# mLSTM on Trainium2: a head's first values and keys begun in the third chunk of the head in front, the second pair's in the first chunk, GLA scans of the last heads behind the gate

## The chip, the cores and the metric

The kernel runs on one core of a Trainium2 chip. The metric is device time in microseconds (us) of one launch, the median of three runs. The engines are named as in the profile: PE (TensorE) with PEld for its weight loads, DVE (VectorE), ACT (ScalarE), POOL (GpSimd), SP (SyncE, which issues the DMAs). Each engine runs its instructions strictly in the order in which they stand in its queue; between engines there are semaphores.

## The reference, cut to what matters

A layer with one projection, two groups of heads and one output projection, on 2048 tokens of width 1024, in float32:

```python
u = rms_norm(x, norm_g)
q_g, k_g, v_g, z_g, r_g, x_m, z_m = split(u @ w_in)
log_a = log_sigmoid(r_g @ w_gla_gate_up + b_gla_gate) / 16      # GLA: 4 heads, dk 128, dv 256
S_t = diag(a_t) S_{t-1} + k_t^T v_t ;  o_g = q_t S_t            # in chunks, b = cumsum(log_a)
o_g = rms_norm(o_g) * silu(z_g)
c_act = silu(causal_conv4(x_m))                                 # mLSTM: 4 heads of 256
q_m, k_m = headwise(c_act, ..), headwise(c_act, ..);  v_m = headwise(x_m, ..)
C_t = f C_{t-1} + i v k^T ;  n_t = f n + i k                    # running-max stabiliser
h_m = C_t q_t / max(|n_t . q_t|, 1)
o_m = (rms_norm(h_m) + mlstm_skip * c_act) * silu(z_m)
return rms_norm(x + concat[o_g, o_m] @ w_out)
```

The cumulative sum of the gates is the `scan` of the text below; `v`, `v1l`, `ctk`, `ctl` are values and keys of the mLSTM.

## The kernel before

Tokens go in four blocks (`b`) of 512, each of four chunks (`c`) of 128. The first stretch of the span, to about 700 us, is the mLSTM of all four blocks; then comes the GLA of all four blocks, to about 1380, then the output projection. A product in float32 is made of three matmuls: each operand is split into a high part and a low part (`uh`/`ul`, `whi`/`wlo`, `v`/`v1l`, `ctk`/`ctl`), the high part by a cast on ACT, the low part by a subtraction on DVE or POOL.

The projections (`pp`, in the GLA part also `pv`) are a long stream of matmuls. PE's order is written out by hand by a small model: generators for the heads' work are advanced between pieces of the stream, `yield x` asks for x us of stream before the next step, `yield "name"` waits until that name is set. At most two heads of the mLSTM are open at a time. `od.wait()` and `od.hold(t)` model a pair of PSUM banks: `hold(t)` says how long after this step its bank is taken to be in use, and `wait` puts stream work ahead until the older of the two banks is taken to be free.

These two banks (`ps_t`, tag `pt`) carry in turn `pqp` (a head's queries), `pma` (its scores), `pmv` (values of a pair of chunks), `pmc` (transposed keys of a pair), and `pt` (the closing transposes of a pair, in `fin_pair`). A tile can be written once the tile two before it has been read. The readers are: of `pma` the scores' split (`A`, lines 788 to 790, ACT, DVE and POOL); of `pmv` `v` on ACT (853) and `v1l` on DVE (854), one of each for each chunk of the pair; of `pmc` `ctk` on ACT (869) and `ctl` on DVE (870); of `pt` two DVE steps into `ost` (805, 806).

A head is `mattn(b, h)` (line 809). After queries and scores it makes the values and keys of its first pair of chunks, `prep_v(0)` and `prep_c(0)`, once the head in front is done; then it goes through its four chunks. In a chunk: the split of the state, `C` (898 on ACT, 899 on DVE); two state updates `pmu` with their DVE step `Tm` (909); the output `pmo`; the split query `qx` of the next chunk (`prep_q`, ACT and POOL); and the norm: `dn`, `r`, a reciprocal on DVE (920 to 922), `jk` with its sum on ACT (925), `rsa` on DVE (220), `rs` on POOL (221), `rs` on DVE (928), `on` on ACT (931). In chunk 0 the second pair's values are made (`prep_v(1)`), in chunk 1 its keys (`prep_c(1)`); chunk 2 is the first to use both. The first head of a block takes its gates from `pkg` and `G` (735).

Order on the other engines is set by a scheduler with priorities (`ahead(tc, ...)`, `at(tc, ...)`), and where `after([...])` stands, as written.

In the GLA part `ggates` makes for each head four scans (1080), one for each chunk, and a copy of the last values `blast` (1083); `z` is gated by `th` (ACT, 580) and `zs` (DVE, 581), whose bank the stream's first `pv` matmul takes over; `zdone[b, 1]` is the `zs` of the block's second tile. One scan, the first of head 2, is ordered after it.

Of the kernel before, what the change touches and what calls it, by code (L numbers as in the profile page):

```python
# [25 lines left out]
H = 4  # L26
# [60 lines left out]
@contextmanager  # L87
def ahead(tc, n):

    tc.cur_priority -= n  # L90
    yield
    tc.cur_priority += n


def at(tc, n):
    def wrap(f):
        def g(*a):
            with ahead(tc, n):
                return f(*a)
        return g  # L100
    return wrap
# [58 lines left out]
def fast_path(ctx, tc, inside, xT, x, w_fm, w_v, w_r, wqT, wkT, wvT, wv, wg, w_up, b_g,  # L160
              norm_g, gla_g, conv_w, conv_b, b_if, ml_g, skip, w_out, fin_g, out):
    nc = tc.nc
    od = Order(tc)
# [646 lines left out]
    def mattn(b, h):  # L810
# [19 lines left out]
            for e in range(2):  # L830
                mm(pa[:, cs], cm[2 * h + e][:, cs], qp[:, e, cs], e == 0, e == 1)
        A = asplit(pa)
        od.hold(0.00)
        yield f"gr{b}"
        wk, wkh, wkl, ga, fl = gts[b]
        if h not in Tm:
# [37 lines left out]
        @at(tc, HPQ)  # L874
        def prep_q(c):
            if c < NC and (b or c):
                qx[c] = gp.tile([P, 2, 2, P], F32R, name="qx", tag="ca", bufs=2)
                split(qx[c][:, 0], qx[c][:, 1], qp[:, :, c * P:(c + 1) * P], QX)

        if (b, h) != (0, 0):  # L880
            yield f"mm{b}_{h - 1}" if h else f"mm{b - 1}_{H - 1}"
        yield from od.wait()
        prep_q(0)
        prep_v(0)
        od.hold(1.80)
        yield from od.wait()
        prep_c(0)
        od.hold(1.10)
        yield 2.10
        on = {}  # L890
        for c in range(NC):
            cs = slice(c * P, (c + 1) * P)
            first = b == 0 and c == 0
            last = b == NB - 1 and c == NC - 1
            if not first:
                Ch, Cl = (gp.tile([P, 2, 258], F32R, name="C", tag="C", bufs=2) for i in range(2))
                with ahead(tc, HPX):
                    nc.scalar.activation(Ch, T, AF.Copy, scale=ga[:, c, h:h + 1])
                    nc.vector.scalar_tensor_tensor(Cl, T, ga[:, c, h:h + 1], Ch.bitcast(F32), op0=ALU.mult, op1=ALU.subtract)
            v1, ctk = kv[c]  # L900
            if not last:
                for e in range(2):
                    pu = ps_u.tile([P, 258], F32, name="pmu", tag="pu")
                    mm3(pu, (ctk[0][:, e, :], ctk[1][:, e, :]), v1, True, True)
                    with ahead(tc, HPT):
                        if first:
                            nc.scalar.copy(T[:, e, :], pu)
                        else:
                            nc.vector.scalar_tensor_tensor(T[:, e, :], T[:, e, :], ga[:, c, h:h + 1], pu, op0=ALU.mult, op1=ALU.add)
                yield 0  # L910
            po = ps_o.tile([P, 258], F32, name="pmo", tag="po")
            mm3(po, (A[:, c, :], A[:, NC + c, :]), v1, True, first)
            if not first:
                for e in range(2):
                    mm3(po, (qx[c][:, 0, e, :], qx[c][:, 1, e, :]), (Ch[:, e, :], Cl[:, e, :]), False, e == 1)
            prep_q(c + 1)
            with ahead(tc, HPN):
                r = sp.tile([P, 1], F32, name="r", bufs=4)
                dn = sp.tile([P, 1], F32, name="dn")
                nc.vector.tensor_scalar(dn, po[:, DV:DV + 1], -1.0, fl[:, c, h:h + 1], op0=ALU.mult, op1=ALU.max)  # L920
                nc.vector.tensor_tensor(r, dn, po[:, DV:DV + 1], op=ALU.max)
                nc.vector.reciprocal(r, r)
                jk = sp.tile([P, DV], BF16, name="jk", bufs=1)
                ss = sp.tile([P, 1], F32, name="ss", bufs=4)
                nc.scalar.activation(jk, po[:, 0:DV], AF.Square, scale=r, accum_out=ss)
                rs = sp.tile([P, 1], F32, name="rs", bufs=4)
                rsqrt(rs, ss, DV)
                nc.vector.tensor_tensor(rs, rs, r, op=ALU.mult)
                o = gp.tile([P, DV], F32, name="on", bufs=4)
                if MON:  # L930
                    nc.scalar.activation(o, po[:, 0:DV], AF.Copy, scale=rs)
                else:
                    nc.vector.tensor_scalar(o, po[:, 0:DV], rs, None, op0=ALU.mult)
            on[c] = o
            yield 0.20
            if c < 2:
                yield from od.wait()
                (prep_v, prep_c)[c](1)
                od.hold(2.10)
            if c < NC - 1:  # L940
                yield 1.90
        od.done.add(f"mm{b}_{h}")
# [101 lines left out]
    def ggates(b):  # L1044
        yield (f"r{b}")
        yield 0.96
        yield from od.wait()
        prr = ps_t.tile([P, TB], F32, name="prr", tag="pt")
        for t in range(NC):
            tr(prr[0:16, t * P:(t + 1) * P], rts[b][:, t, :])  # L1050
        nc.vector.tensor_copy(rstk[0:16, :], prr[0:16, :])
        nc.vector.tensor_copy(rstk[64:80, :], rstk[0:16, :].bitcast(F32))
        nc.vector.tensor_tensor(rstk[32:48, :], prr[0:16, :], rstk[0:16, :].bitcast(F32), op=ALU.subtract)
        od.hold(1.70)
        yield 1.50
        prs = [gq.tile([P, 2, TB + 4], F32, name=f"bc{p}", tag=f"x{p}") for p in range(2)]
        for h in range(H):
            yield from od.wait()
            pg = ps_t.tile([P, TB], F32, name="pg", tag="pt")
            mm(pg, upk[:, h * P:(h + 1) * P], rstk, True, True)  # L1060
            nc.vector.tensor_scalar(prs[h // 2][:, h % 2, :TB], pg, bg[:, h:h + 1], -GCLIP, op0=ALU.add, op1=ALU.max)
            od.hold(0.98)
            yield 0
        chain = []
        for p in range(2):
            w = prs[p][:, :, :TB]
            chain.append(nc.scalar.activation(w, w, AF.Exp, scale=-1.0, accum_out=esum[:, b, p:p + 1]))
        for p in range(2):
            w = prs[p][:, :, :TB]
            chain.append(nc.scalar.activation(w, w, AF.Ln, bias=1.0))  # L1070
        after(chain)
        yield GY0
        for h in range(H):
            if h == 2 and f"za{b}_1" not in od.done:
                yield f"za{b}_1"
            w = prs[h // 2][:, h % 2, :TB]
            w3 = w.rearrange("p (c t) -> p c t", t=P)
            with ahead(tc, HYG):
                for c in range(NC):
                    sc = nc.vector.tensor_tensor_scan(w3[:, c], ones, w3[:, c], 0.0, op0=ALU.mult, op1=ALU.add)  # L1080
                    if h == 2 and c == 0:
                        after([zdone[b, 1], sc])
                nc.vector.tensor_copy(blast[:, b, h, :].unsqueeze(2), w3[:, :, P - 1:P])
            bc[b, h] = w
            od.done.add(f"gg{b}_{h}")
            yield GY1
# [694 lines left out]
```

## Time and profile before

| | |
|---|---|
| median of 3 runs | 1698.77 us (1696.33 to 1699.51) |
| profiled execution, its own time | 1694.07 us |
| its span | 1691.8 us |
| mean granted clock of PE | 0.989 |
| PE / PEld busy | 95% / 80% of the span |
| DVE / ACT / POOL busy | 56% / 41% / 26% |
| PE matmuls | 8840 |

Times in the rows are microseconds from the start of the span. Matmuls are pipelined: the length of a row runs into the next one, so the pace is read from start to start. What stands in brackets at the end of a row is the idle time of the engine before it and what ended that idle time. The granted clock of PE is 1.00 at 2.4 GHz and 0.50 at 1.2 GHz.

### The profile page before, as it was taken

What the parts mean: (1) busy time and instruction counts of PE and PEld (TensorE: products, weight loads), DVE (VectorE), ACT (ScalarE), POOL (GpSimd) and SP (SyncE); (2) the same over time, 40 slices, a digit from 0 to 9 for tenths busy, and PEclk for the clock granted to TensorE, in tenths of its full rate; (3) what the DMA queues carried; (4) which work ended last, traced back from release to release, by engine and by line L of the source; (5) the groups of instructions that cost most, each with busy time, mean ns of one, the idle gap of its engine ahead of it and who ended that gap; (6) DMA issues with size and microseconds to landing.
All of it is one profiled execution on the core that took longest, in us unless ns stands there. A gap on an engine that the chain in (4) does not pass through costs nothing.

```text
span 1691.8 us, 25558 instructions
## 1 busy us (share of the span) xinstructions
PE 1613.0 (95%) x8840; PEld 1354.0 (80%) x8840; DVE 954.7 (56%) x2125; ACT 695.3 (41%) x1486; POOL 444.9 (26%) x422
## 2 busy tenths in 40 slices
PE   7989899999999999899999999999999999999997
PEld 5767777877888788788888988888889877887775
DVE  4966776775667576834442434233523556567663
ACT  4666754554555455413231323132422433243331
POOL 3434321220121024344302120302031214223330
PEclk9999999999999999999999999999999999999999
DMA  8677667636664766666868586758575575573441
GB/s 268 200 266 241 230 219 236 199 107 211 200 199 145 221 196 203 213 241 202 301 212 298 187 299 202 255 175 288 194 261 193 175 250 195 168 249 133 163 144 65
DMA packets 221258, 355.42 MB, mean 210 GB/s; under 512 B 24368, under 2 KB 58160, under 8 KB 221120
## 3 DMA queue, kind: packets, MB, share of 16 engines
q1 hardware_dynamic: 221120, 353.70, 62.9%
q8 instruction: 72, 1.18, 0.3%
q14 instruction: 66, 0.54, 0.1%
HBM read 253.86 MB, written 102.89 MB: 211 GB/s over the span
## 4 chain that ended last, share of the span: by engine, by line
PE 45%; DVE 5%; DMA 3%; issue 3%; ACT 2%; POOL 2%; SPq 0%; POOLq 0%; DVEq 0%; ACTq 0%
PE py L191 16%; PE pp L191 16%; PE pv L191 9%; PE po L191 2%; DVE bc L1080 1%; PE pu L191 1%; DMA wlo<-w_dr 1%; PE pt L201 1%; PE pa L191 1%; POOL ring L1217 1%; DMA f<-q_dr 0%; DMA ring<-in_w_out 0%; DMA whi<-w_dr 0%; DVE as L215 0%; DVE yh L1312 0%
## 5 line engine op out<-in xcount | busy, mean ns | idle before, releaser
L191 PE MATMUL pp<-uh,whi 128*128 128x512 f32 x1008 | 420.8, 417 | 12.7 <-ACT whi L214 6.1
L191 PE MATMUL pp<-uh,wlo 128*128 128x512 f32 x1008 | 400.6, 397 | 0.2 <-POOL wlo L215 0.2
L191 PE MATMUL pp<-ul,whi 128*128 128x512 f32 x1008 | 400.3, 397 | 0.5 <-DVE ul L404 0.4
L191 PEld LDWEIGHTS pp<-uh,whi 128*128 128x128 f32 x1008 | 192.3, 191 | 53.0 <-ACT whi L214 6.1
L191 PEld LDWEIGHTS pp<-uh,wlo 128*128 128x128 f32 x1008 | 191.4, 190 | 47.6 <-DMA wlo<-w_dr 0.9
L191 PEld LDWEIGHTS pp<-ul,whi 128*128 128x128 f32 x1008 | 191.9, 190 | 39.7 <-issue 4.5
L215 POOL TENSOR_TENSOR wlo<-wraw,whi 128x512 fp32r<-128x512 f32 (+1 forms) x97 | 133.8, 1385 | 158.0 <-ACT whi L214 54.4
L1217 POOL TENSOR_TENSOR ring<-ring,ring 128x512 f32<-128x512 f32 x77 | 106.2, 1384 | 240.6 <-DMA ring<-in_w_out 112.4
L191 PE MATMUL pv<-whi,uh 128*128 128x256 f32 (+1 forms) x512 | 148.9, 291 | 10.6 <-DVE zs L581 8.5
L191 PE MATMUL pv<-wlo,uh 128*128 128x256 f32 (+1 forms) x512 | 145.6, 284 | 0.8 <-DMA wlo<-w_dr 0.5
L191 PE MATMUL pv<-whi,ul 128*128 128x256 f32 (+1 forms) x512 | 145.6, 284 | 0.0
L191 PE MATMUL py<-f,as 128*128 128x512 f32 x540 | 134.2, 400 | 8.7 <-DVE yf L1312 3.9
L214 ACT CAST as<-ring 128x512 fp32r<-128x512 f32 x105 | 65.0, 621 | 168.7 <-PE py L191 117.8
L191 PEld LDWEIGHTS py<-f,as 128*128 128x128 f32 x540 | 103.1, 192 | 34.3 <-ACT f L214 8.5
L215 POOL TENSOR_TENSOR qx<-qp,qx 128x256 fp32r<-128x256 f32 x60 | 55.7, 931 | 272.0 <-ACT qx L214 272.0
L191 PEld LDWEIGHTS pv<-whi,uh 128*128 128x128 f32 x512 | 97.1, 190 | 13.3 <-DVE zs L581 9.3
L191 PEld LDWEIGHTS pv<-wlo,uh 128*128 128x128 f32 x512 | 97.0, 189 | 1.9 <-DMA wlo<-w_dr 1.8
L191 PEld LDWEIGHTS pv<-whi,ul 128*128 128x128 f32 x512 | 97.2, 190 | 0.7
L215 DVE TENSOR_TENSOR as<-ring,as 128x512 fp32r<-128x512 f32 x105 | 85.2, 814 | 12.9 <-ACT as L214 12.2
L645 DVE SCALAR_TENSOR_TENSOR c<-xm,cw,c 128x512 f32<-128x512 f32 x96 | 78.2, 822 | 14.1 <-ACT c L643 13.4
L221 POOL TENSOR_TENSOR grs<-rsa,nhalf 128x2 f32<-128x2 f32 x32 | 23.4, 732 | 199.0 <-DVE rsa L220 177.8
L985 DVE TENSOR_TENSOR vl<-pv,v 128x256 fp32r<-128x256 f32 x56 | 23.5, 422 | 79.6 <-ACT v L983 79.6
(341 smaller groups left out, 3151.0 us busy)
## 6 DMA issues: line engine op xcount, KB each, us to landing
whi<-w_dr SPq DMA_DIRECT2D x212, 256.0 KB, 3.8
wlo<-w_dr SPq DMA_DIRECT2D x212, 256.0 KB, 4.2
wraw<-in_w_fm SPq DMA_DIRECT2D x80, 256.0 KB, 4.1
w_dr<-whi SPq DMA_DIRECT2D x76, 256.0 KB, 3.4
w_dr<-wlo SPq DMA_DIRECT2D x76, 256.0 KB, 3.3
o_dr<-ost SPq DMA_DIRECT2D x64, 256.0 KB, 3.4
ring<-o_dr SPq DMA_DIRECT2D x60, 256.0 KB, 3.1
ul<-u_dr SPq DMA_DIRECT2D x56, 256.0 KB, 4.3
```

Source lines behind the costliest of these rows:

```text
L191: nc.tensor.matmul(o, l, r, start=start, stop=stop, **k)
L201: nc.tensor.transpose(o, i, ident)
L214: nc.scalar.copy(hi, raw)
L215: (nc.gpsimd if "l" in pool else nc.vector).tensor_tensor(lo, raw, hi.bitcast(F32), op=ALU.subtract)
L221: nc.gpsimd.tensor_tensor(dst, a, nhalf.broadcast_to(list(src.shape)), op=ALU.pow)
L645: nc.vector.scalar_tensor_tensor(ca, xt[:, 1 + j:1 + j + TB], cw[:, t, j:j + 1], ca, op0=ALU.mult, op1=ALU.add)
L985: nc.vector.tensor_tensor(vl[b, h][t // 2][:, t % 2, :], pv[:, :DV], vv[b, h][:, t, :].bitcast(F32), op=ALU.subtract)
L1080: sc = nc.vector.tensor_tensor_scan(w3[:, c], ones, w3[:, c], 0.0, op0=ALU.mult, op1=ALU.add)
L1217: nc.gpsimd.tensor_tensor(o, a, b, op=ALU.subtract)
```

## The change

Four edits; the instructions of every engine stay the same in kind and number.

1. The second pair's values and keys are both made in chunk 0 (before: values in chunk 0, keys in chunk 1).
2. A head's first values and keys may start once the chunk 2 of the head in front has been written out (name `mp`), not only when that head is done (name `mm`). The first split query, `prep_q(0)`, comes after the head in front is done.
3. The hold of the scores' bank goes from 0.00 to 2.60, those of values and keys from 1.80, 1.10 and 2.10 to 2.20.
4. In `ggates` all scans of heads 2 and 3 are ordered after `zdone[b, 1]`, where before only the first scan of head 2 was.

```diff
         A = asplit(pa)
-        od.hold(0.00)
+        od.hold(2.60)
...
+        front = f"{b}_{h - 1}" if h else f"{b - 1}_{H - 1}"
         if (b, h) != (0, 0):
-            yield f"mm{b}_{h - 1}" if h else f"mm{b - 1}_{H - 1}"
+            yield "mp" + front
         yield from od.wait()
-        prep_q(0)
         prep_v(0)
-        od.hold(1.80)
+        od.hold(2.20)
+        yield 0
         yield from od.wait()
         prep_c(0)
-        od.hold(1.10)
+        od.hold(2.20)
         yield 2.10
+        if (b, h) != (0, 0) and "mm" + front not in od.done:
+            yield "mm" + front
+        prep_q(0)
...
-            if c < 2:
-                yield from od.wait()
-                (prep_v, prep_c)[c](1)
-                od.hold(2.10)
+            if c == 0:
+                for prep in (prep_v, prep_c):
+                    yield from od.wait()
+                    prep(1)
+                    od.hold(2.20)
+                    yield 0
+            if c == 2:
+                od.done.add(f"mp{b}_{h}")
...
-                    if h == 2 and c == 0:
+                    if h > 1:
                         after([zdone[b, 1], sc])
```

What this does to the order is shown at three places. The first is PE in the first head of block 1. Before, the second pair's keys (`pmc_3187`) stand one chunk's output behind `pmo_3152` of chunk 1, and `pmu_3209` of chunk 2 follows after nine stream matmuls:

```order
L191 MATMUL pmo_3152<-C_3138,qx_3079 128x258
L191 MATMUL pp_3108<-uh4_1786,whi_2969 128x512
...
L201 MATMUL pmc_3187<-ident_71,c0_2207 128x128
L201 MATMUL pmc_3187<-ident_71,c1_2219 128x128
...
L191 MATMUL pp_3108<-uh7_1830,whi_2969 128x512
L191 MATMUL pp_3108<-ul7_1831,whi_2969 128x512
L191 MATMUL pp_3108<-uh7_1830,wlo_2970 128x512
L191 MATMUL pmu_3209<-v1_3117,ctk_3188 128x258
L191 MATMUL pmu_3209<-v1l_3118,ctk_3188 128x258
L191 MATMUL pmu_3209<-v1_3117,ctl_3189 128x258
```

In after the same head has the values (`pmv_3119`) and keys (`pmc_3132`) of the second pair in chunk 0, then chunk 1 (`pmu_3158`, `pmo_3168`), and only then `pmu_3237` of chunk 2:

```order
L191 MATMUL pmv_3119<-wvs_124,xm0_2224 128x128 x4
L201 MATMUL pmc_3132<-ident_71,c0_2229 128x128
L201 MATMUL pmc_3132<-ident_71,c1_2241 128x128
...
L191 MATMUL pp_3063<-uh2_1737,whi_2906 128x512
...
L191 MATMUL pmu_3158<-v1_3022,ctk_3035 128x258
...
L191 MATMUL pmo_3168<-v1_3022,A_2839 128x258
...
L191 MATMUL pp_3063<-uh5_1861,whi_2969 128x512
...
L191 MATMUL pmu_3237<-v1_3120,ctk_3133 128x258
L191 MATMUL pmu_3237<-v1l_3121,ctk_3133 128x258
L191 MATMUL pmu_3237<-v1_3120,ctl_3134 128x258
```

So a whole chunk has moved between the keys and their first use. On ACT, at the same place, before had the cast `ctk_3188` behind `jk_3170` of chunk 1's norm:

```order
L898 ACTIVATE C_3205<-Tm0_1111,ga_2911 128x516
L214 CAST qx_3229<-qp_2773 128x256
L925 ACTIVATE jk_3170,ss_3171<-pmo_3152,r_3165 128x256
L869 CAST ctk_3188<-pmc_3187 128x512
L931 ACTIVATE on_3178<-pmo_3152,rs_3173 128x256
L580 ACTIVATE th_3248<-pp_3108 128x512
```

In after (whose lines from 880 on are numbered a few higher) the cast is `ctk_3133`:

```order
L929 ACTIVATE jk_3106,ss_3107<-pmo_3088,r_3101 128x256
L853 ACTIVATE v1_3120<-pmv_3119,wk_2931 128x256
L869 CAST ctk_3133<-pmc_3132 128x512
L935 ACTIVATE on_3114<-pmo_3088,rs_3109 128x256
L853 ACTIVATE v1_3120<-pmv_3119,wk_2931 128x256
L902 ACTIVATE C_3233<-Tm0_1114,ga_2934 128x516
```

It stands between the norm steps of chunk 0 and among the two value casts of its pair. The second place is PE at the change from that head to the next one. Before, the new head's values (`pmv_3342`) and keys (`pmc_3361`) follow the last output of the old head (`pmo_3298`) and the first closing transposes (`pt_3330`), and the second `pt_3376` comes after them:

```order
L191 MATMUL pmo_3298<-C_3284,qx_3229 128x258
...
L201 MATMUL pt_3330<-ident_71,on_3095 128x128 x2
L201 MATMUL pt_3330<-ident_71,on_3178 128x128 x2
L191 MATMUL pmv_3342<-wvs_124,xm1_2412 128x128 x4
...
L201 MATMUL pmc_3361<-ident_71,c2_2417 128x128
L201 MATMUL pmc_3361<-ident_71,c3_2518 128x128
...
L201 MATMUL pt_3376<-ident_71,on_3245 128x128 x2
L201 MATMUL pt_3376<-ident_71,on_3321 128x128 x2
```

In after they stand between the old head's chunk 2 (`pmo_3247`) and its chunk 3 (`pmu_3307`):

```order
L191 MATMUL pmo_3247<-C_3233,qx_3178 128x258
...
L191 MATMUL pmv_3278<-wvs_124,xm1_2412 128x128 x4
L201 MATMUL pmc_3291<-ident_71,c2_2417 128x128
L201 MATMUL pmc_3291<-ident_71,c3_2529 128x128
...
L191 MATMUL pp_3225<-uh2_1737,whi_2998 128x512
L191 MATMUL pp_3225<-ul2_1738,whi_2998 128x512
L191 MATMUL pp_3225<-uh2_1737,wlo_2999 128x512
L191 MATMUL pmu_3307<-v1_3120,ctk_3133 128x258
```

The new head's preparation has moved one chunk forward, and no stream matmul separates `pmv` and `pmc`. The third place is DVE in the GLA part, block 1. Before, eight scans of the first two heads (`bc_9891`) and seven of the last two (`bc_9892`) stand ahead of the second `zs`:

```order
L581 SCALAR_TENSOR_TENSOR zs<-th,pp 128x512
L1080 SCALAR_TENSOR_TENSOR bc_9891<-ones,bc_9891 128x128 x5
L1083 COPY blast<-bc_9891 128x4
L1080 SCALAR_TENSOR_TENSOR bc_9891<-ones,bc_9891 128x128 x3
L1080 SCALAR_TENSOR_TENSOR bc_9892<-ones,bc_9892 128x128
L1083 COPY blast<-bc_9891 128x4
L1080 SCALAR_TENSOR_TENSOR bc_9892<-ones,bc_9892 128x128 x2
L1022 TENSOR_SCALAR bc_9891<-bc_9891 128x512
L1080 SCALAR_TENSOR_TENSOR bc_9892<-ones,bc_9892 128x128 x4
L581 SCALAR_TENSOR_TENSOR zs<-th,pp 128x512
```

In after:

```order
L581 SCALAR_TENSOR_TENSOR zs<-th,pp 128x512
L1088 SCALAR_TENSOR_TENSOR bc_9891<-ones,bc_9891 128x128 x5
L1091 COPY blast<-bc_9891 128x4
L1088 SCALAR_TENSOR_TENSOR bc_9891<-ones,bc_9891 128x128 x3
L1030 TENSOR_SCALAR bc_9891<-bc_9891 128x512
L1091 COPY blast<-bc_9891 128x4
L1185 COPY el_10543<-eb 128x1
L581 SCALAR_TENSOR_TENSOR zs<-th,pp 128x512
L1088 SCALAR_TENSOR_TENSOR bc_9892<-ones,bc_9892 128x128 x4
```

No scan of the last two heads stands ahead of the second `zs` any more.

## Rows read from the trace of the kernel before

**Rows 1.** The page's table of busy time: engine, us, share of the span, instructions.

```profile
PE 1613.0 (95%) x8840; PEld 1354.0 (80%) x8840; DVE 954.7 (56%) x2125; ACT 695.3 (41%) x1486; POOL 444.9 (26%) x422
```

**Rows 2.** PE's waits: what waited, for what, us in total, times, longest.

```profile
PE pmu L191 <- DVE ctl L870: 9.7, 13, 1.2
PE pv L191 <- DVE zs L581: 8.5, 4, 3.0
PE pmu L191 <- ACT ctk L869: 7.3, 7, 2.9
...
PE pt L201 <- DVE v1l L854: 4.5, 4, 1.8
...
PE pqp L191 <- DVE G L735: 3.1, 4, 2.3
...
PE pqp L191 <- DVE v1l L854: 0.8, 1, 0.8
```

**Rows 3.** Timeline of PE, block 1, first head: start, us, engine, line, operation.

```profile
289.32 0.60 PE L201 MATMUL pmc<-ident,c 128*128 128x128 f32 x4
...
291.89 0.39 PE L191 MATMUL pmu<-v,ctk 128*128 128x258 f32 x1
292.12 0.28 PE L191 MATMUL pmu<-v1l,ctk 128*128 128x258 f32 x1
293.32 0.39 PE L191 MATMUL pmu<-v,ctl 128*128 128x258 f32 x1 [0.92 <-DVE ctl L870]
```

**Rows 4.** Timeline of ACT, the same head.

```profile
290.80 0.47 ACT L925 ACTIVATE jk<-pmo,r 128x256 bf16<-128x256 f32 x1
...
291.26 0.58 ACT L869 CAST ctk<-pmc 128x512 fp32r<-128x512 f32 x1
```

**Rows 5.** Timeline of DVE, the same head.

```profile
292.50 0.16 DVE L928 TENSOR_TENSOR rs<-rs,r 128x1 f32<-128x1 f32 x1 [0.95 <-POOL rs L221]
292.58 0.69 DVE L870 TENSOR_TENSOR ctl<-pmc,ctk 128x512 fp32r<-128x512 f32 x1
```

**Rows 6.** PE behind a wait; windows: PE, PEld, DVE, ACT, POOL, PEclk, DMA, GB/s.

```profile
128.88 0.28 PE L191 MATMUL pmu<-v,ctk 128*128 128x258 f32 x1
129.00 0.35 PE L191 MATMUL pmu<-v1l,ctk 128*128 128x258 f32 x1
...
132.54 0.40 PE L191 MATMUL pp<-uh,whi 128*128 128x512 f32 x1
...
129.07:132.48 3.41, 3.41 (x15) 3.22 (x15) 2.48 (x7) 1.57 (x4) 1.74 (x2) 0.50 0.92 316
...
719.58:722.99 3.41, 3.41 (x19) 3.41 (x18) 0.00 (x0) 0.49 (x2) 0.00 (x0) 0.50 0.00 0
```

**Rows 7.** GLA, block 1: timelines of ACT, DVE and PE.

```profile
883.18 0.58 ACT L580 ACTIVATE th<-pp 128x512 f32<-128x512 f32 x1
...
883.86 1.36 DVE L1080 TENSOR_TENSOR_SCAN bc<-ones,bc 128x128 f32<-128x128 f32 x4
885.14 0.66 DVE L581 SCALAR_TENSOR_TENSOR zs<-th,pp 128x512 f32<-128x512 f32 x1
...
885.85 0.39 PE L191 MATMUL pv<-whi,uh 128*128 128x256 f32 x1 [1.69 <-DVE zs L581]
```

**Rows 8.** Block 0, longest wait of the closing transposes: timelines of PE and ACT.

```profile
190.18 0.48 PE L191 MATMUL pp<-uh,whi 128*128 128x512 f32 x1
...
195.42 0.63 PE L201 MATMUL pt<-ident,on 128*128 128x128 f32 x4 [1.77 <-DVE v1l L854]
...
191.22 0.63 ACT L356 ACTIVATE xtok<-xtok 128x512 f32<-128x512 f32 x1 [2.32 <-DMA xtok<-in_x]
```

**Rows 9.** Block 0, queries after the gates: timeline of PE.

```profile
93.08 0.70 PE L191 MATMUL pqp<-c,wqk 128*128 128x512 f32 x1 [2.29 <-DVE G L735]
```

**Rows 10.** Block 0: timelines of DVE and POOL at the same time.

```profile
124.30 1.24 DVE L857 CAST v1l<-wkl 128x4 fp32r<-128x4 f32 x1
...
124.22 1.29 POOL L215 TENSOR_TENSOR wlo<-wraw,whi 128x512 fp32r<-128x512 f32 x1 [1.11 <-ACT whi L214]
```

## Prediction

> **What bounds the kernel now.** I read the page's busy table first: TensorE (PE) is busy for 95% of the span and its loads 80% [rows 1]. The matmuls are the same before and after, so only PE's idle time can shrink, plus what a lowered clock adds. The next view is PE's waits by what ended them [rows 2]. Of the waits that the change can reach, the largest are those of `pmu` (the state update of a chunk) for the split keys: 9.7 us for the low part `ctl` in 13 waits and 7.3 us for the high part `ctk` in 7, 17.0 us in 20 rows. Then `pv<-zs` in the GLA part, 8.5 us in four, `pt<-v1l`, 4.5 us in four, and `pqp<-G`, 3.1 us in four. Third I read the timelines of one ordinary head, the first of block 1, on PE, ScalarE (ACT) and VectorE (DVE). All 20 `pmu` waits sit at the third chunk, where the second pair's keys are first used. There PE transposes the keys at 289.32, runs nine projection matmuls, and wants `ctk` at 291.89 [rows 3]. On ACT the cast `ctk` starts only at 291.26, behind `jk` of the second chunk's norm [rows 4]; on DVE `ctl` starts at 292.58, behind `rs` of the same norm, which stood 0.95 us for POOL [rows 5]. So 2.1 us of PE work (nine at 0.23) must cover a chain of some 4 us (289.32 to 293.27). That is the stall.
>
> An idle of 0.92 us costs more than 0.92: from 292.12 to 293.32 is 1.20 us where 0.12 is the step [rows 6], so 0.16 comes on top. And three of these waits are followed by a lowered clock. After the wait of block 0 the granted clock was 0.50 for 3.41 us, the lower of the two levels [rows 6]: from 128.88 to 132.54 PE took 3.66 us for twelve matmuls of 0.12 and three of 0.23, 2.13 us of work, so 1.5 us was lost. Four such stretches of 3.41 us at 0.50 concern the change; [rows 6] has the first and the last: three behind `pmu` waits, one behind the first `zs` wait.
>
> **The change part by part.** The profiled execution took 1694.07 us (span 1691.8); the median of the three runs is 4.7 us higher. I sum against the profile and add 4.7 at the end. Every engine gets the same instructions, so only waits are summed.
>
> 1. Second pair's keys in the first chunk. The order of after puts the whole second chunk between `pmc` and the `pmu` that wants it: fifteen matmuls of 0.12 and twelve of 0.23, 4.6 us more, 6.7 in all (6.4 to 7.0 over the sixteen heads). On ACT `ctk` now stands behind `jk` and a `v` of the first chunk, on DVE `ctl` behind `rs` and one `v1l`. Even a chain with the longest wait of both kinds [rows 2] would be covered: 2.1 + 2.9 + 1.2 is 6.2. So all 20 waits go: 17.0 + 20 x 0.16 = **20.2 us**, and their three clock drops, 3 x 1.5 = **4.5 us**. What comes late next is the bank, point 3.
>
> 2. GLA scans behind `zs`. In block 1 PE waits 1.69 us for `zs`; DVE holds it back with scans of the last two heads at 0.34 each (1.36 for four), seven of them ahead of it, while its other input `th` was done at 883.76 [rows 7]. With the scans behind, `zs` can start at 883.76 and end 0.66 later, so PE starts near 884.45 and 1.4 of 1.69 goes. The like wait of block 2 gives the same; the waits of blocks 2 and 3 are 8.5 - 3.0 - 1.7 = 3.8 together, of which seven scans (2.4 us) can return all of the larger one; I take 1.4 and 2.0. In block 0 six scans, 2.0 us, stand in the way of a wait of 3.0; I take 1.9. Sum **6.7 us** and the drop of **1.5** behind the wait of 3.0, since behind the three shorter ones (1.7 to 2.1) the clock stayed up and 1.1 would be left. Cover: the scans now run beside PE's value projection; the keys of the last two heads want them several microseconds later. If that cover is gone, their `eb` comes late by at most these 2.4 us a block, which would return the whole term (a rival below).
>
> 3. Banks of PSUM. Transposes, values, scores, `pqp` and the closing `pt` share two banks, so each tile waits until the tile two before it is read. After, `pmv` and `pmc` of a pair follow each other with nothing or three matmuls between them, and then `pt` comes: from `pmv` to the `pt` that wants its bank lie 2.5 us of PE work at eight places (around second and third heads) and 3.6 at eight others. Before, these were 1.8 to 2.5 and 3.2. The bank is free when both `v1l` are done; while `pt` waits, the projection and the next `pmu` stand behind it in PE's order. The worst chain of the trace took 5.2 us: PE was past `pmv` at 190.18, `pt` started at 195.42 after a wait of 1.77, since `v` stood on ACT behind `xtok`, which had waited 2.32 for a DMA [rows 8]. Walking the engines' orders of after with durations of the profile (`v` 0.47, `v1l` 0.48, `rs` of POOL 0.6), the second `v1l` ends 0.6 to 0.9 after `pt` wants it in second heads (1.5 in block 0), 0.3 to 1.0 in third heads: 4.2 and 3.2 us with 0.16 each, 7.4; for the DMA-fed disturbances, one more of 1.9 in block 0. That is 9.3, where before shows 4.5 + 0.8 (four `pt` and one `pqp`, [rows 2] for the four) + 5 x 0.16 = 6.1. Net **+3.2 us**. The bounds: no wait at all, -6.1; each of the sixteen as the worst, 16 x 1.93 = 31, +25. I stay near the walk, because most of the sixteen places before, with the same chain, show no wait.
>
> 4. The scores' hold. `pqp` no longer stands right behind `pkg` in the first head of a block but behind twelve projection matmuls, 2.8 us, more than either wait. In block 0 it waited 2.29 for `G` [rows 9], in the other three blocks 0.3 each [rows 2]. All of 3.1 us goes; with 4 x 0.16, **3.7 us**. The second `pma` goes back by as much, which nothing waits for.
>
> 5. Values and keys of the next head in the third chunk. This happens only in second heads; in the others the limit of two heads keeps the start near where it was. From `pmc` to the first `pmu` before 1.8 to 2.5, after 2.9 to 3.6 in second heads; the trace shows no wait at a first chunk, so this gives 0. `qx`, moved behind the end of the head in front, stands on ACT in time; the first chunk of the head wants it 2 us after it is issued, and its cost is 0.39 + 0.93. I take 0, between 0 and 4 x 1.
>
> Sum: -20.2 - 4.5 - 6.7 - 1.5 + 3.2 - 3.7 = -33.4. New small waits that I can't see, an ACT or DVE queue in another order in 16 heads, get 0.2 each: +3.2. **-30 us**: 1664 by the profile, 1669 by the median.
>
> A rule that speaks of DVE: the row of a 128x4 cast into `v1l` took 1.24 us in block 0 while POOL ran a `wlo` of 1.29 [rows 10]; the other casts take some 0.2. The Trainium skill, "SBUF — State Buffer", section "Who interferes with whom", says that a DVE copy or cast in its two-port mode and GpSimd lock each other out for a whole instruction; the trace agrees, 1.24 against 0.2. The casts stand in the chain of point 3, so by that rule every place there that meets a `wlo` would be a microsecond later, and the term +3.2 would grow by about one for each.
>
> **The rivals.**
> - *More than forecast.* No bank wait appears, and the walk is too dark: -33.4 - 9.3 = -43 at most; 1656 to 1662. For: most `pt` of before do not wait. Against: the `pmv` to `pt` spacing shrinks in third heads. Chance 0.12.
> - *The two banks are the limit, and the waits move.* With the eight 2.5 us places at the worst seen (1.93) and the eight others at 1.2 (1.03 and less is what the other three `pt` waits are, plus 0.16), 15.4 + 9.6 = 25 instead of 9.3, so 16 of the 30 is given back: 1685; half of that, 1677. The rule of the Trainium skill, "Perfetto Trace Analysis", section "Optimization Strategy", that the same gap repeated can mean too little PSUM for the next tile, names this case; here the repeated gap of before has another cause, the queue behind `jk` and `rs`. Chance 0.2.
> - *GLA gives nothing*, because the late scans hold back the last heads' `eb`: 8 less, 1677. Against: in the trace `eb` of those heads is wanted after the value projection. Chance 0.08.
> - *Slower.* The chain from `pmv` to the second `v1l` is made long at all sixteen places, since ACT now has `jk`, two `v` and `ctk` together. Price: with the chain at 5.2 us, eight places lose 2.7 + 0.16 and a clock drop of 1.5 each, 35, eight lose 1.6 + 0.16, 14: 49 in all, against gains of 36.6 + 6.1 = 43. So 1705, and it decides from a mean chain of about 4.8 us. Against: one chain in sixteen took 5.2. Chance 0.05; the stretch of the same mechanism that ends within 0.2%, a chain of 4.6 to 5.0, has 0.05.
> - *The change doesn't do what it says* is excluded by the orders, which show `ctk` and the scans moved.
>
> **How the numbers follow.** The forecast, 1662 to 1675, has 0.5; more 0.12; banks 0.2; GLA 0.08; same 0.05; slower 0.05. The range 1657 to 1688 leaves out half of "more" and the last two, 0.16. About 0.2%, 3.4 us, is what a measurement can tell from no change. Faster is 0.5 + 0.12 + 0.2 + 0.08 = 0.90.
>
> **What would show it.** No `pmu` wait for `ctk` or `ctl` at third chunks and no clock of 0.50 between 100 and 700 us (point 1); `pv<-zs` under 2 us in all (point 2); `pt<-v1l` between 5 and 10 us (point 3: over 20, banks); no `pqp<-G` (point 4). It would be wrong if the `pt` or `pmv` rows carry more than 25 us, or if `pmu` waits for `C` or `Tm` instead.

## The result, and the profile after

The changed kernel takes 1682.4 us (median of 5 runs, 1681.0 to 1688.3) against 1698.8 before: a ratio of 0.9911, 95% interval 0.9893 to 0.9929, 16 us faster. The prediction had 1669, a forecast of 1662 to 1675 and a range of 1657 to 1688. So the direction and the range held, the forecast did not, and about half of the 30 us is missing. The profiled execution after has a span of 1679.9 us, 12 less than the one before.

Where the time went is read by stage. The borders are the starts of the first `pkg` of each mLSTM block, the first `pg` of the GLA part and the first `py` of the output projection on PE's timeline (us, worked out from those starts; one execution each):

| | ahead of block 0 | block 0 | block 1 | block 2 | block 3 | GLA | rest | median |
|---|---|---|---|---|---|---|---|---|
| before | 89.8 | 169.6 | 159.6 | 157.8 | 126.9 | 644.2 | 343.9 | 1698.8 |
| after | 89.1 | 169.7 | 157.7 | 156.5 | 125.1 | 636.4 | 345.5 | 1682.4 |

The GLA part gives 7.8 us, blocks 1 to 3 of the mLSTM together 5.0, block 0 nothing.

PE's time in a stretch is its busy time plus its idle time, and the first grows when the clock is lowered (behind 209.37 after, the stream's matmuls start 0.43 us apart at 0.50, and 0.23 apart once it is 1.00 again). The windows of block 0, then of blocks 1 to 3, before and after (stretch, its length, PE busy, the other engines, PEclk, DMA share, GB/s):

```profile
89.84:259.42 169.58, 155.39 (x854) 126.45 (x852) 118.01 (x297) 104.60 (x230) 59.16 (x59) 0.98 0.73 240
89.08:258.75 169.67, 158.27 (x853) 128.66 (x852) 118.50 (x297) 104.08 (x230) 59.95 (x59) 0.96 0.73 240
```

```profile
259.42:703.70 444.28, 429.59 (x2500) 358.64 (x2498) 308.13 (x845) 231.32 (x492) 106.25 (x123) 1.00 0.59 188
258.75:698.03 439.28, 425.39 (x2500) 358.01 (x2498) 309.39 (x845) 230.17 (x492) 102.46 (x123) 1.00 0.60 189
```

In block 0 PE's idle time did fall, from 14.2 to 11.4 us, but its busy time grew by 2.9: the clock was at 0.50 for four times 3.41 us, where before it was twice. In blocks 1 to 3 the idle time hardly fell, from 14.7 to 13.9: there the waits moved, and 4.2 of the 5.0 us are busy time. By the prices of the prediction, an estimate, the drop that went (1.5) and the 0.16 behind each of 14 key waits (2.2) make 3.7 of these.

Over the whole span PE's busy time on the page fell by 4.7 us against [rows 1]; the rest of the 12 was idle time:

```profile
PE 1608.3 (96%) x8840; PEld 1351.8 (80%) x8840; DVE 956.2 (57%) x2125; ACT 693.0 (41%) x1486; POOL 441.6 (26%) x422
```

PE's waits after, by what ended them (what waited, for what, us in total, times, longest), beside [rows 2]:

```profile
PE pt L201 <- DVE ctl L870: 8.8, 10, 1.4
...
PE pmo L191 <- DVE C L903: 4.7, 5, 2.0
...
PE pmu L191 <- DVE Tm L913: 2.9, 4, 2.1
...
PE pv L191 <- DVE zs L581: 1.9, 3, 1.2
PE pmc L201 <- DVE xm L632: 1.8, 2, 0.9
...
PE pmc L201 <- DVE ost L805: 1.3, 1, 1.3
...
PE pmu L191 <- DVE ctl L870: 1.0, 2, 0.7
...
PE pmu L191 <- ACT ctk L869: 0.9, 1, 0.9
```

The 17.0 us of `pmu` waits for the keys are 1.9 now, `pv<-zs` fell from 8.5 to 1.9, and `pqp<-G` is gone. In their place stand `pt<-ctl` with 8.8 and, in small pieces, waits for the state (`C`, `Tm`) and for banks of `pmc`: 4.7 + 2.9 + 1.8 + 1.3, 10.7 us, where before had 0.6 of them. (The row `pmc<-xm` names a copy that has nothing to do with the bank; `ost`, which reads it, stands just ahead of that copy on DVE in both cases.)

GLA, block 1, as [rows 7] (timelines of ACT, DVE and PE): `zs` now stands behind nothing but its own input `th`, which ends at 875.40, and PE waits 0.36 in place of 1.69.

```profile
874.82 0.58 ACT L580 ACTIVATE th<-pp 128x512 f32<-128x512 f32 x1
...
875.43 0.69 DVE L581 SCALAR_TENSOR_TENSOR zs<-th,pp 128x512 f32<-128x512 f32 x1
...
876.17 0.39 PE L191 MATMUL pv<-whi,uh 128*128 128x256 f32 x1 [0.36 <-DVE zs L581]
```

The new wait is read at the change from the first to the second head of block 1. The next head's `pmv` and `pmc` are issued in chunk 2 of the old head, and PE comes to the old head's `pt` after three stream matmuls, chunk 3 and three more (timelines of PE, ACT and DVE):

```profile
294.81 0.60 PE L201 MATMUL pmc<-ident,c 128*128 128x128 f32 x4
...
299.49 0.66 PE L201 MATMUL pt<-ident,on 128*128 128x128 f32 x4 [0.86 <-DVE ctl L870]
300.36 0.36 PE L191 MATMUL pmu<-v,ctk 128*128 128x258 f32 x1 [0.22 <-DVE Tm L913]
...
297.76 0.47 ACT L935 ACTIVATE on<-pmo,rs 128x256 f32<-128x256 f32 x1 [0.99 <-DVE rs L932]
298.13 0.58 ACT L869 CAST ctk<-pmc 128x512 fp32r<-128x512 f32 x1
...
297.56 0.16 DVE L932 TENSOR_TENSOR rs<-rs,r 128x1 f32<-128x1 f32 x1 [0.98 <-POOL rs L221]
...
298.74 0.69 DVE L870 TENSOR_TENSOR ctl<-pmc,ctk 128x512 fp32r<-128x512 f32 x1 [0.62 <-ACT ctk L869]
299.35 0.47 DVE L854 SCALAR_TENSOR_TENSOR v1l<-pmv,wk,v 128x256 fp32r<-128x256 f32 x1
299.74 0.86 DVE L913 SCALAR_TENSOR_TENSOR Tm<-Tm,ga,pmu 128x258 f32<-128x258 f32 x2
```

`ctk` still stands on ACT behind a norm's step, now `on`, which waits for `rs`, which waits for POOL; `ctl` waits on DVE for `ctk`; and behind `ctl` and `v1l` stands, at 299.74, the old head's state step `Tm`. The chain of [rows 3] to [rows 5] is not shorter than before: from `pmc` to the end of `ctl` it takes 4.6 us (294.81 to 299.43), where it took 3.95. It only has another reader: `pt`, since the scheduler gave `pt` the bank of `pmc` (PE starts 0.06 us after `ctl` ended at 299.43, and before the second `v1l` ended at 299.82), not that of `pmv`. So the two banks are not always taken in turn: here `pt` waits for the tile just before it, and not for the one two before.

### The profile page after: what moved, and what is told of

Its sections match the earlier page's. It is cut to its first block, busy times and chain, and to the rows that moved or that the text cites. A ratio compares the mean times of both kernels' runs of the same rounds, so it can differ in the third digit from the quotient of the medians.

```text
span 1679.9 us, 25563 instructions
## 1 busy us (share of the span) xinstructions
PE 1608.3 (96%) x8840; PEld 1351.8 (80%) x8840; DVE 956.2 (57%) x2125; ACT 693.0 (41%) x1486; POOL 441.6 (26%) x422
```

## The experiments

All stage times in one table, in the form of the one above; what each run changes follows.

| run | ahead | block 0 | block 1 | block 2 | block 3 | GLA | rest | median |
|---|---|---|---|---|---|---|---|---|
| e1, second pair alone | 88.9 | 174.7 | 155.2 | 154.5 | 123.1 | 642.9 | 344.2 | 1690.6 |
| e2, third chunk alone | 90.8 | 168.7 | 160.5 | 163.3 | 134.0 | 649.1 | 343.5 | 1709.8 |
| e3, scores' hold alone | 87.8 | 172.0 | 157.3 | 157.3 | 126.6 | 643.1 | 343.7 | 1699.3 |
| e4, scans alone | 88.8 | 173.4 | 159.4 | 157.2 | 127.8 | 636.7 | 345.7 | 1686.6 |
| e5, after without third chunk | 88.7 | 168.8 | 155.3 | 155.5 | 123.3 | 640.3 | 344.2 | 1679.5 |
| e6, second pair and scans | 91.4 | 172.2 | 155.7 | 154.5 | 123.4 | 636.2 | 344.4 | 1682.1 |
| e7, after, values' hold 4.40 | 89.4 | 166.8 | 161.0 | 159.2 | 125.8 | 634.1 | 346.8 | 1686.4 |
| e8, after without second pair | 89.5 | 172.2 | 159.7 | 159.9 | 130.1 | 634.3 | 345.1 | 1692.8 |
| e9, after, low parts in pieces | 88.6 | 168.2 | 158.7 | 156.2 | 125.8 | 636.7 | 344.1 | 1681.4 |
| e10, after, no weight split | 90.1 | 163.7 | 158.7 | 156.3 | 125.0 | 637.1 | 344.2 | 1675.5 |
| e11, before, no weight split | 90.0 | 158.5 | 159.9 | 157.2 | 129.1 | 647.6 | 344.9 | 1687.2 |
| e12, second pair in blocks 1 to 3 | 90.5 | 174.6 | 155.3 | 156.1 | 124.1 | 634.1 | 344.3 | 1680.2 |

How far a stage can be trusted: before and e4 have the same order in block 0 on every engine, and took 169.6 and 173.4 there; e3 and e12 likewise, 172.0 and 174.6. So block 0 scatters by some 4 us from run to run; blocks 1 to 3 repeat within about 1 (before and e4, e1 and e6). The GLA stage takes 634.1 to 640.3 in the nine versions that have the scans' edit and 642.9 to 649.1 in the five without: the gain is clear, and its size is known to some 6 us.

### The four parts alone

**e1.** Before, with:

```diff
-            if c < 2:
-                yield from od.wait()
-                (prep_v, prep_c)[c](1)
-                od.hold(2.10)
+            if c == 0:
+                for prep in (prep_v, prep_c):
+                    yield from od.wait()
+                    prep(1)
+                    od.hold(2.20)
+                    yield 0
```

> Before with one edit: the second pair's values and keys both in chunk 0. Theory A (the early start of the next head in the third chunk brings the bank waits of the changed kernel): the 20 waits of pmu for ctk and ctl, 17.0 us, fall to under 3 us, pt waits stay near the 4.5 us of before, and the time falls by 12 to 20 us. Theory B (putting both preparations into chunk 0 is itself what moves the waits, by crowding VectorE and ScalarE there): the same pmu waits go, but pt<-ctl and pmo<-C come with 8 to 14 us, and the time falls by only 2 to 6 us.

Measured: 1690.6, 0.9960 (0.9946 to 0.9975), 7 us faster; between the two theories. By stage it is both: blocks 1 to 3 gave 4.4, 3.2 and 3.9 us, 11.5 together, of the 11.8 us that the chunk-2 waits cost there (9.6 in 14 waits, with 0.16 each) and the 1.5 of one clock drop; block 0 got 5.1 longer. PE's waits:

```profile
PE pt L201 <- DVE v1l L854: 6.9, 6, 2.0
PE pmu L191 <- DVE Tm L909: 4.1, 3, 2.8
PE pqp L191 <- DVE G L735: 3.2, 4, 2.4
...
PE pmu L191 <- DVE ctl L870: 0.3, 1, 0.3
```

The key waits are gone (0.3), there is no `pt<-ctl`, and all of the 4.1 us for `Tm` lies in block 0.

**e2.** Before, with the start of the next head's preparation moved:

```diff
-            yield f"mm{b}_{h - 1}" if h else f"mm{b - 1}_{H - 1}"
+            yield "mp" + front
...
-        prep_q(0)
         prep_v(0)
-        od.hold(1.80)
+        od.hold(2.20)
+        yield 0
...
+        if (b, h) != (0, 0) and "mm" + front not in od.done:
+            yield "mm" + front
+        prep_q(0)
...
+            if c == 2:
+                od.done.add(f"mp{b}_{h}")
```

> Before with one edit: a head's first values and keys may start after chunk 2 of the head in front, the first split query after its end, holds 2.20. Theory A: pt<-ctl waits appear with some 8 us and the chunk-2 waits stay at 17 us, so 4 to 10 us slower. Theory B: nothing of weight at the head changes, within 3 us of before.

Measured: 1709.8, 1.0067 (1.0046 to 1.0088), 12 us slower. The direction is theory A's, the wait is not: it is `pmc` that waits, for the scores to be read (PE's waits):

```profile
PE pmu L191 <- DVE ctl L870: 11.2, 14, 2.1
PE pmc L201 <- DVE A L789: 8.6, 4, 2.8
...
PE pmu L191 <- ACT ctk L869: 4.9, 4, 2.9
```

With a hold of 0.00 the order does not know that the scores' bank is in use, and puts `pmc` behind `pma` with only `pmv` between them. In the changed kernel the hold of 2.60 is there and this wait is not among its rows. The GLA stage of this execution is 5 us longer than before's too. Its clock is lowered at 730.95 for 6.83 us, from within the first `zs` wait (it ends at 731.91), and at 1154.2; before has two stretches of 3.41 there, at 719.58 and 1269.12. Nothing in the edit explains these 5 us.

**e3.** Before, with:

```diff
         A = asplit(pa)
-        od.hold(0.00)
+        od.hold(2.60)
```

> Before with one edit: the scores' hold 2.60. Both theories: the four waits of pqp for G (3.1 us) go, the rest stays, 2 to 4 us faster; if block 0 gives it back later, 0 to 1.

Measured: 1699.3, 1.0005 (0.9992 to 1.0018): nothing. `pqp<-G` is gone, and in this execution as many microseconds stand elsewhere, in the keys and in `pt`:

```profile
PE pmu L191 <- DVE ctl L870: 12.4, 15, 2.6
...
PE pt L201 <- DVE v1l L854: 4.7, 7, 1.0
PE pt L201 <- ACT on L931: 1.9, 1, 1.9
```

**e4.** Before, with `if h == 2 and c == 0:` made `if h > 1:`.

> Before with one edit: all scans of the last two GLA heads after the second zs. Both theories: pv<-zs falls from 8.5 to about 2 us and the clock drop at 719.58 goes: 7 to 9 us faster, all of it between the GLA gates of the first and the last block; the mLSTM stretch unchanged.

Measured: 1686.6, 0.9928 (0.9907 to 0.9949), 11 us by the medians; the GLA stage of the trace gives 7.5, with `pv<-zs` at 1.9 us and no lowered clock behind it. This part acts by itself and as costed.

Alone, the four make -7.0 + 12.3 + 1.7 - 11.0 = -4.0, together -16.4: they are not independent. The third-chunk start needs the scores' hold: e8 has both, and there no `pmc` waits for the scores.

### The changed kernel with one part taken back, and combinations

**e5.** The changed kernel without the edit of e2.

> The changed kernel without its third-chunk edit (first pair and first split query as before). Theory A (the third-chunk start gives back part of what the second pair gains, by pt waiting for the bank of pmc): pt<-ctl, 8.8 us in ten waits after the change, falls under 2, the blocks 1 to 3 of the mLSTM take some 4 us each less than before (as in the run with the second pair alone, 155.2, 154.5) and the time is 4 to 8 us below the changed kernel, about 1675 to 1679. Rival (the edits need each other: the scores' hold and the second pair alone crowd another bank): equal to the changed kernel within 2 us.

Measured: 1679.5, 0.9895 (0.9856 to 0.9935), 3 us below the changed kernel and the lowest median of the versions that compute the layer, though the two intervals overlap. Blocks 1 to 3 are 2.4, 0.9 and 1.9 shorter than after. PE's waits:

```profile
PE pt L201 <- DVE v1l L854: 5.9, 6, 1.6
PE pmc L201 <- DVE ost L805: 5.3, 3, 2.4
PE pmo L191 <- DVE C L899: 3.3, 5, 1.4
```

`pt<-ctl` is down to one wait of 1.5, so the third-chunk start does give back some 5 us in blocks 1 to 3, as theory A had it in kind; the 4 to 8 us that it said of the time are not reached. The 5.3 of `pmc<-ost` lie in block 0.

**e6.** Before, with the edits of e1 and e4 only.

> Before with two edits: second pair in chunk 0, and the scans behind zs. If the parts add: -7.0 (second pair alone) and -11.0 (scans alone) make 18, some 1680; by the stage times of the traces (blocks 1 to 3 -11.5, GLA -8) 20 in the undisturbed stages, with block 0 open by 5 either way. With the scores' hold left out, pqp<-G keeps its 3 us.

Measured: 1682.1, 0.9908 (0.9873 to 0.9943), 15 us faster, 3 short of the parts' sum and the same as the whole change. Two of the four edits carry all of it, as far as intervals of 6 us either way can tell.

**e7.** The changed kernel with more of PE's work between the next head's keys and the old head's `pt`:

```diff
         prep_v(0)
-        od.hold(2.20)
+        od.hold(4.40)
...
                     prep(1)
-                    od.hold(2.20)
+                    od.hold(4.40 if prep is prep_v else 2.20)
```

> The changed kernel with the hold of the values' bank 4.40 in place of 2.20 at both places, so that more of PE's work stands between the keys and the closing transposes. Theory A (bank): pt<-ctl falls from 8.8 to under 2 us, the blocks 1 to 3 get 2 to 3 us shorter each, the time 5 to 9 us below the changed kernel. Rival (the state's chain on VectorE is what limits a chunk now): the waits reappear as pmo<-C and pmu<-Tm, the time stays within 2 us.

Measured: 1686.4, 0.9935 (0.9911 to 0.9959), 4 us slower than the changed kernel by the medians, though the intervals overlap; blocks 1 to 3 are 3.3, 2.7 and 0.7 longer. Theory A falls here, and the rival has the wait right, if not the time (within 2 us). `pt<-ctl` is gone altogether, and the wait stands one step on. The first of PE's waits is now

```profile
PE pmu L191 <- DVE Tm L913: 7.2, 4, 2.3
```

and at the same head change as above the timelines of PE and DVE read

```profile
298.48 0.41 PE L191 MATMUL pmu<-v,ctk 128*128 128x258 f32 x1 [2.30 <-DVE Tm L913]
...
295.69 0.16 DVE L932 TENSOR_TENSOR rs<-rs,r 128x1 f32<-128x1 f32 x1 [0.97 <-POOL rs L221]
...
296.86 0.69 DVE L870 TENSOR_TENSOR ctl<-pmc,ctk 128x512 fp32r<-128x512 f32 x1 [0.62 <-ACT ctk L869]
297.47 0.48 DVE L854 SCALAR_TENSOR_TENSOR v1l<-pmv,wk,v 128x256 fp32r<-128x256 f32 x1
297.86 0.87 DVE L913 SCALAR_TENSOR_TENSOR Tm<-Tm,ga,pmu 128x258 f32<-128x258 f32 x2
```

DVE's order is `rs`, `v1l`, `ctl`, `v1l`, and only then the old head's `Tm` of its last chunk. The next `pmu` needs the banks that `Tm` reads. In the changed kernel `pt` met this chain first and waited 0.86, and `pmu` found it nearly done (0.22); with `pt` out of the way `pmu` meets it and waits 2.30, more than before and with a lowered clock behind it. So the bank of `pt` was the place of the wait and not its cause. At this head change the cause is the next head's preparation in DVE's queue, between a norm that waits for POOL and the old head's state. The Trainium skill, "Perfetto Trace Analysis", section "Optimization Strategy", takes a repeated gap as a possible sign of too little PSUM; the ten like waits of the changed kernel looked so, and this run speaks against it for them. No run gave these tiles one more bank.

**e8.** The changed kernel without the edit of e1.

> The changed kernel without its second-pair edit (values in chunk 0, keys in chunk 1 as before). Theory A: the chunk-2 waits are back with some 17 us and pt waits stay, blocks 1 to 3 take 2 to 5 us each more than before; the GLA keeps its gain of 8: about the time of before, plus 0 to 6. Rival: the second pair gives nothing in the company of the other edits, within 2 us of the changed kernel.

Measured: 1692.8, 0.9978 (0.9961 to 0.9994). Blocks 1 to 3 take 2.0, 3.4 and 5.0 us more than in the changed kernel, `pmu` waits 12.1 + 4.9 us for the keys again. So theory A is right about the keys. It had the time at that of before or up to 6 us above, and it is 4 below; its `pt` waits did not stay (3.0 us in one, for `on`). In their place stands a wait for the copied queries that neither before nor after has:

```profile
PE pma L191 <- ACT qp L821: 8.1, 5, 2.6
```

### Why block 0 gave nothing

**e9.** The changed kernel, with POOL's subtraction for a new weight cut:

```diff
-                      split(hi, lo, raw, "" if self.got < 4 else WM if self.got < NB * 4 * KT else WG)
+                      m = "" if self.got < 4 else WM if self.got < NB * 4 * KT else WG
+                      if m == WM:
+                          (nc.vector.tensor_copy if "h" in m else nc.scalar.copy)(hi, raw)
+                          for z in range(0, n, 128):
+                              nc.gpsimd.tensor_tensor(lo[:, z:z + 128], raw[:, z:z + 128], hi[:, z:z + 128].bitcast(F32), op=ALU.subtract)
+                      else:
+                          split(hi, lo, raw, m)
```

> The changed kernel with POOL's subtraction of each new weight's low part cut into pieces of 128 columns, same work. Question: why block 0 gains nothing (169.6 us from its gates to the next block's before, 169.7 after, 168.8 to 174.7 in the other versions). Theory P (DVE instructions that stand for the whole of POOL's 1.3 us make block 0's chains long): the DVE instructions of block 0 that take over 0.3 us more than usual, 13 us in 20, fall to under 7, block 0 gets 3 to 6 us shorter. Theory Q (block 0's own work, the splits of new weights in ACT's and POOL's queues, fills the queues whatever its pieces): block 0 stays within 3 us, or gets longer by POOL's added pieces.

Measured: 1681.4, 0.9904 (0.9874 to 0.9934), the changed kernel's time. The long DVE instructions did go: counting for each DVE instruction of block 0 what it took over the lower quartile of its group (same line, tiles and shape, over the whole span), and of these the ones over 0.3 us, 13.3 us in 20 became 3.7 in 9. Block 0 got 1.5 shorter, less than its scatter. So theory P has its mechanism and not its price. The mutual blocking that the Trainium skill states ("SBUF — State Buffer", section "Who interferes with whom") is what these 9.6 us agree with; the prediction's microsecond for each place that meets a `wlo` is not seen in the time.

**e10 and e11.** The changed kernel and the one before, with new mLSTM weights not split from the 20th piece on (their two parts are loaded from places written earlier, so what is computed is not the layer):

```diff
+                if kind == "fm" and self.LATE + 4 <= self.sent < NB * 4 * KT:
+                    self.have[self.sent] = (a, q, self.sent)
...
+                    if isinstance(raw, tuple):
+                        for t in (hi, lo):
+                            nc.sync.dma_start(t.bitcast(F32), w_dr[raw[2] % 2, int(t is lo), :, :512])
+                    else:
```

> The changed kernel without the splits of new mLSTM weights from the 20th piece on: their high and low parts are loaded from places written earlier (the values are not the weights, so what follows is not the layer). ACT loses some 27 casts of 0.62 us, POOL as many subtractions of 1.38, most of them in block 0. Theory Q: block 0 falls to some 160 us or less, the length of the other blocks plus the first head's extra, its waits for C, Tm and pmc under 6 us. Rival (block 0 is long for another reason, DMA or the row sums of x): stays above 166.

> The kernel before with the same leaving out as the run ahead. Theory Q: with the splits gone the change has in block 0 the effect it was expected to have, so block 0 here is 5 to 10 us longer than in the run ahead, with its pmu waits for ctk and ctl at some 6 us; the whole difference between the two is 20 to 25 us less what the bank gives back (5 to 8). Rival: the difference in block 0 is under 2 us, as with the splits.

Measured: 1675.5 and 1687.2. The splits are worth 6 us in block 0 of the changed kernel and 11 in that of the kernel before (169.6 to 158.5). Block 0 of e10 lies between theory Q's 160 and the rival's 166. The second half of theory Q is wrong with its sign: without the splits the kernel before has the shorter block 0, 158.5 against 163.7. So the splits lengthen block 0, but they are not what hides the change's gain there. The edit also adds loads: the DMA share of block 0 rises from 0.73 to 0.87 (changed kernel) and 0.88. Of the 5.2 us between the two runs, 4.0 are PE's busy time (151.8 and 155.8): the clock is at 0.50 for three times 3.41 us in e10 (at 133.28 and, twice as long, at 201.54), and never in e11.

**e12.** As e5, with block 0's second pair as before (`if b == 0 and c < 2:` the old lines, `if b and c == 0:` the new ones).

> The version without the third-chunk edit (second pair in chunk 0, scores' hold, scans behind zs), with block 0's second pair as before: the edit acts in blocks 1 to 3 alone. Theory X (in block 0 the edit gives nothing and costs nothing, since PE meets other late chains there): block 0 within 169 to 173 us, blocks 1 to 3 at 155, 155.5 and 123, the time within 3 us of the version with the edit in all blocks (1679.5). Theory Y (in block 0 it costs some 5 us, as between the two runs without the weights' splits, 163.7 against 158.5): 3 to 6 us faster than that, 1674 to 1677. Theory Z (it gains there, hidden by scatter): 3 to 6 us slower, 1683 to 1685.

Measured: 1680.2, 0.9904 (0.9884 to 0.9925), against 1679.5: nearest to theory X, with block 0 at 174.6 a little above its range. The intervals, 3.5 us either way here and 6.7 for e5, do not exclude the 3 to 6 us of theories Y and Z. The edit's gain is that of blocks 1 to 3, and in block 0 it can't be told from nothing.

## Why the prediction was right or wrong, point by point

**Right: what the removed waits were worth where they were removed.** Point 1 said that all 20 waits for the keys go; 17.0 us became 1.9, three waits in block 0, and e1 and e8 show that this edit does it and is worth 11.5 us (alone) in blocks 1 to 3, where the working had 11.8 and one drop of 1.5. The third-chunk start costs some 5 us there (e5, and e8 against before), and less than half is left, 5.0: PE's idle time in these blocks is 8.0 us in e1, 10.2 in e5 and 13.9 in the changed kernel, against 14.7 before. Point 2 had 8.2 us with the clock; the GLA stage gave 7.8 and e4 alone 7.5. That it comes so near is in part luck: the stage scatters by some 6 us, and a lowered stretch at 1269.12 that no point counted is gone too.

**Right in size by luck, wrong in its reason: the banks.** Point 3 had 9.3 us of `pt` waits; the trace has 8.8 + 0.6 in 11 waits, with 0.16 each 11.2. But it walked the second `v1l` of `pmv`'s bank, and ten of the eleven waits are for `ctl` of `pmc`'s. The sign it gave, `pt<-v1l` between 5 and 10 us, is not there at all. And e7 shows that taking the bank's wait away returns nothing.

**Wrong: points 3 and 5 asked who waits for the moved tiles, not who stands behind their readers.** The step "I take 0" of point 5, with the 0.2 a head for "new small waits that I can't see" (3.2 us), is the term that failed. Waits for `C`, `Tm` and the banks of `pmc` are 10.7 us in 12 waits against 0.6 before, 12.6 us with 0.16 each. `v1l` and `ctl` that moved ahead on PE moved ahead on DVE too, and there the state of the head in front queues behind them. The prediction had named this as a sign of being wrong, "if `pmu` waits for `C` or `Tm` instead"; it came in part, `pmu` for `Tm` with 2.9 us, `pmo` for `C` with 4.7.

**Wrong: the clock in the mLSTM.** Point 1 counted 4.5 us for three drops of 3.41 us. After, block 0 has four times 3.41 us at 0.50, two of them in one stretch of 6.83 from 206.07 on: it begins 1.1 us behind the wait of 2.10, and the wait of 1.96 lies within it (timelines of PE, DVE and POOL, then the three windows, with PEclk 0.50):

```profile
204.97 0.39 PE L191 MATMUL pmu<-v,ctk 128*128 128x258 f32 x1 [2.10 <-DVE Tm L913]
...
208.13 1.44 PE L191 MATMUL pmo<-C,qx 128*128 128x258 f32 x5 [1.96 <-DVE C L903]
...
203.38 1.14 DVE L645 SCALAR_TENSOR_TENSOR c<-xm,cw,c 128x512 f32<-128x512 f32 x1
204.44 0.47 DVE L913 SCALAR_TENSOR_TENSOR Tm<-Tm,ga,pmu 128x258 f32<-128x258 f32 x1
...
207.24 0.16 DVE L932 TENSOR_TENSOR rs<-rs,r 128x1 f32<-128x1 f32 x1 [1.61 <-POOL rs L221]
207.32 0.75 DVE L903 SCALAR_TENSOR_TENSOR C<-Tm,ga,C 128x516 fp32r<-128x516 f32 x1
...
205.18 1.53 POOL L215 TENSOR_TENSOR wlo<-wraw,whi 128x512 fp32r<-128x512 f32 x1 [1.21 <-ACT whi L214]
206.66 0.55 POOL L221 TENSOR_TENSOR rs<-rsa,nhalf 128x1 f32<-128x1 f32 x1
```

```profile
134.39:137.80 3.41, 3.23 (x14) 3.18 (x15) 3.07 (x12) 1.92 (x7) 2.20 (x3) 0.50 0.49 183
189.00:192.41 3.41, 3.41 (x16) 3.04 (x15) 2.01 (x9) 2.54 (x7) 1.14 (x2) 0.50 0.69 239
206.07:212.90 6.83, 4.87 (x15) 4.00 (x15) 3.70 (x12) 3.17 (x8) 1.69 (x3) 0.50 0.33 111
```

`Tm` stands behind the convolution of the next block (`c`), and `C` behind `rs`, which stood on POOL behind the low part of a weight. Block 1's drop (371.42) is gone, as forecast. The sign that point 1 gave, no clock of 0.50 between 100 and 700 us, did not come: there is one stretch of 3.41 us more than before in the mLSTM, where point 1 had three fewer: at its price of 1.5 each, 6 us short.

**Wrong: point 4.** The waits of `pqp` for `G` went, 3.1 us, and e3 shows that the time did not; in its execution block 0 lost in `pt` and the keys what the queries gained.

**The sum.** By the profiled executions 18 of the 30 us are missing. An estimate from the rows: the new small waits 12.6 in place of 3.2, the clock 6, the keys that still wait 2.4 (1.9 with 0.16 each), the banks 1.9 over the walk. That is some 20 us, about what is missing.

**What stays open.** Point 1 had 8.5 us of waits and two drops in block 0, point 4 another 2.4; none came back as time. In this pair of executions 2.8 us came back as idle time, and two more stretches of lowered clock took them; that the change brings these stretches is not shown, since before and e4, with one order, differ by one stretch too. e9 and e10 speak against the blocking between DVE and POOL and the weights' splits as the whole reason. The traces show other late chains in every version of it (`Tm`, `C`, `ost`, `on`), but no single one, and a scatter of 4 us; the 5 us by which the change lengthens block 0 without the splits rest on one execution each.

Of the rivals, "the banks are the limit, and the waits move" has the right time (1677 to 1685) and half the right cause: the waits did move, but e7 speaks against the banks as the limit. "GLA gives nothing" and "slower" did not come; that the third-chunk start alone is 12 us slower, with 8.6 us of waits for the scores' bank, none of them had.

## What to carry to other kernels

When a step is moved forward on the engine that bounds, list its readers on the other engines and then what stands behind those readers there: a wait removed from one place goes to the next instruction that needs the same queue. A wait named after a bank is tested by giving the bank more time; if another wait takes its place in full, look at the queue of the bank's reader for the cause. Parts of a change that share a planner are costed together, and a stage that scatters by 4 us from run to run is no place to count on 10.

## What the runs showed of the hardware

A POOL subtraction cut into four pieces of 128 columns took 9.6 us off the long DVE instructions of one block (13.3 to 3.7), which agrees with [rows 10], and the kernel's time did not notice.
